# A two-layer hybrid S5 / RetNet / GLA backbone on one core: S5 of the last layer as two streams, a new queue order for the opening, norms rounded straight from PSUM, and SBUF copies in the pack

## The chip, the cores and the metric

One core of a Trainium2 chip runs the whole program in one launch. The metric is device time in microseconds (us). Three runs of the kernel before gave 1385.05, 1386.57 and 1379.94 us, a median of 1385.05 us. The engines are TensorE (PE, matmuls, with PEld as its weight loads), VectorE (DVE), ScalarE (ACT), GpSimd (POOL) and SyncE (SP, which issues most DMAs). Each engine runs its own list of instructions in order, and waits on the others by semaphores.

## The reference, cut to what matters

All numbers are float32. There are 256 context tokens and 256 latent tokens, 1024 channels, two layers:

```python
for l in range(2):
    need_ctx = l < 1                       # the last layer computes no context output
    m_l = split((silu(c) @ w_mod[l] + b_mod[l]), 6);  m_c = split(silu(c_ctx) @ w_mod[l] + b_mod[l], 6)
    p_l = split_in(modulate(rms_norm(x, norm_mix[l]), m_l[0], m_l[1]) @ w_in[l])
    p_c = split_in(modulate(rms_norm(ctx, norm_mix[l]), m_c[0], m_c[1]) @ w_in[l])
    s5_c, s5_l = s5_branch(p_c[0], p_l[0], ...)        # 16 groups of 16 channels, 64 complex states, two directions
    ret_c, ret_l = retnet_branch(p_c[1:5], p_l[1:5], ...)
    gla_c, gla_l = gla_branch(p_c[5:11], p_l[5:11], ...)
    x = x + m_l[2] * (sum_b(sigmoid(p_l[11 + b]) * (y_b @ w_br[b])) @ w_out[l])
    x = x + m_l[5] * swiglu(modulate(rms_norm(x, norm_ffn[l]), m_l[3], m_l[4]), w_ffn_in[l], w_ffn_out[l])
    if need_ctx: ...                                   # the same two steps for ctx
return rms_norm(x, norm_final)
```

Here `modulate(h, shift, scale)` is `h * (1 + scale) + shift`, so no matmul with `w_in[l]` can start before the two rows `m[0]` and `m[1]` are there, which are themselves products with `w_mod[l]`.

## The kernel before, in words

Activations stand transposed in one tile `rb`: 128 channels of a group by tokens, four token tiles of 128 (two of context, two of latent). Every float32 product is made of three matmuls (`mm3`): each operand is split into a high part `hi` (a rounding copy on ACT) and a low part `lo` (a subtraction on DVE), and hi*hi, hi*lo and lo*hi are added up in a PSUM bank `b`. Weights come as 512 KB tiles `raw` by DMA from SP, are split on ACT and DVE into `hi` and `lo`, and go to PE. A line of the profile names the helper that issued an instruction: L243 is `mm_` (matmul), L253 a transpose on PE, L228 `act`, L231 `tt` (two tensors), L234 `stt`, L238 and L240 `ts`, L593 the copy `perm` of the pack, L273 the weight DMA. The pools hand out buffers; a tile framework with priorities decides in which order each engine's instructions stand, so one edit can move others.

The parts that the change touches, in the order of time:

**The opening (0 to 65 us).** `mod_chunk(c)` computes the shift and scale for 256 of the 1024 channels, in four chunks: two DMAs of 1 MB of `w_mod`, 64 matmuls with 32 columns held in PE (`b<-arena,sil`), a copy of the rows on ACT, a transpose, and three small DVE operations. `norm_chunk(c)` transposes those channels of the four normalised token tiles (8 transposes), and multiplies and adds on DVE (four operations of 128x512), rounds on ACT (one copy of 128x1024) and subtracts on DVE (128x1024) to fill `rb`. `pack_mms(c)` then multiplies with one chunk of the weights `w_in` that feed S5's input and the GLA and RetNet q and k: 24 matmuls of 128x512. The three functions are called for c = 0, 1, 2, 3 in turn. Behind the four chunks come `pack_out`, which copies the four banks (ACT) and writes a permuted copy (`perm`, DVE) that goes out by DMA, `load_params2` and `s5_tables`, small parameter work.

**The pack of layer 1 (around 970 us).** `pack_out(lean=True)` does the same for layer 1; `perm` reads the PSUM bank, and the bank comes free when both the ACT copy and `perm` have read it.

**S5 of layer 1 (970 to 1126 us).** Three generators are woven: `weave("rsg")` calls in turn one step of RetNet (`r`), of S5 (`s`) and of GLA (`g`); in between, `tick`-like steps of the merge gates, large matmul groups on 512 columns, fill PE. `s5_core` works in two halves of 8 groups, one after the other in one generator, with four steps each: load, 16 matmuls of 128x64 (X), rotation, scan and unrotation to the states S (DVE, POOL), read-out of 24 matmuls of 32x128 and ACT copies to `yt`. After the weave `s5_out` transposes `yt` and runs GELU and GLU.

**The norm before the FFN of layer 1 (1183 to 1192 us).** `out_tok` gives the residual rows of two latent token tiles; per tile a square and a mean (ACT), a power (POOL), a scaling (DVE, L238), 8 transposes on PE, then `norm_t`: per half of four transposes two ACT and two DVE affine operations of 128x128 into a float32 tile, one ACT rounding copy of 128x512, one DVE subtraction of 128x512. `ffn_in_tok` then multiplies with `w_ffn_in`, `tok_mms` with both token tiles inside the loop over channels.

## Time and profile before

| | |
|---|---|
| median of three runs | 1385.05 us |
| profiled execution, its own time | 1389.15 us |
| its span, first to last instruction | 1387.1 us |
| mean granted TensorE clock | 0.986 of full |
| PE busy | 1332.2 us (96%) |
| DVE busy | 909.6 us (66%) |
| ACT busy | 579.1 us (42%) |
| DMA engines, mean | 184 GB/s |

The profiled execution took 1389.15 us, 2.05 us more than its span and 4.1 us more than the median of the three runs. PE is busy in 96% of the span, so the whole idle time of PE is 54.9 us; the places where PE stands still, and the few where its clock is halved, are what is left besides the matmuls themselves.

### The profile page before, as it was taken

The numbers are of one execution on the slowest core, as the hardware profiler recorded it, in microseconds if no ns is written. First come the engines' busy times: TensorE is split into PE (matmuls) and PEld (weight loads), VectorE is DVE, ScalarE is ACT, GpSimd is POOL, SyncE is SP. The second block draws the span as 40 slices with busy tenths as digits, with TensorE's granted clock in tenths as the row PEclk, the third lists the DMA queues.
The fourth block names the chain that finished last, engine by engine and source line by source line (L and its number), as shares of the span: only waits on it lengthen the run. The fifth ranks groups of instructions, "written<-read, shape, count | busy, mean of one in ns | idle before, by whom it ended". The sixth has DMA issues, their size and how long they took to land.

```text
span 1387.1 us, 20296 instructions
## 1 busy us (share of the span) xinstructions
PE 1332.2 (96%) x7723; PEld 1082.7 (78%) x7723; DVE 909.6 (66%) x1395; ACT 579.1 (42%) x920; POOL 73.7 (5%) x115
## 2 busy tenths in 40 slices
PE   4899999999999999999999999999999989899997
PEld 3788888777767778788777777898987867788886
DVE  4579682849879665535455687764696688655555
ACT  3367352333432233222222345544456544544453
POOL 3310000002000020000000000000000010000000
PEclk9999999999999999999999999999999989999999
DMA  9743455677877565633333787654655646465653
GB/s 308 205 123 106 153 167 165 228 220 236 280 245 216 200 184 170 215 92 106 119 115 116 250 310 245 197 158 122 181 160 189 199 145 213 149 194 187 213 183 106
DMA packets 202584, 255.63 MB, mean 184 GB/s; under 512 B 20704, under 2 KB 153100, under 8 KB 201976
## 3 DMA queue, kind: packets, MB, share of 16 engines
q1 hardware_dynamic: 189032, 228.05, 52.6%
q10 hardware_dynamic: 10240, 20.39, 4.1%
q0 software_dynamic: 3216, 5.91, 1.7%
q8 instruction: 61, 1.00, 0.3%
q14 instruction: 35, 0.29, 0.1%
HBM read 231.00 MB, written 23.30 MB: 183 GB/s over the span
## 4 chain that ended last, share of the span: by engine, by line
PE 81%; DMA 8%; DVE 5%; issue 2%; ACT 2%; SPq 1%; POOL 0%; DVEq 0%; ACTq 0%; POOLq 0%
PE b L243 79%; DMA wm<-in_w_mod_dram 4%; PE b L253 2%; DVE arena L231 1%; DVE zone L234 1%; DVE lo L231 1%; DMA arena<-in_w_mod_dram 1%; DMA raw<-in_w_in_dram 1%; ACT arena L228 1%; DMA arena<-udr 1%; ACT hi L228 1%; DMA arena<-sw 1%; DMA arena<-in_ctx_dram 0%; DMA raw<-in_w_ffn_out_dram 0%; DMA rb<-k 0%
## 5 line engine op out<-in xcount | busy, mean ns | idle before, releaser
L243 PE MATMUL b<-hi,rb 128*128 128x512 f32 (+2 forms) x1752 | 535.5, 383 | 5.5 <-DVE arena L593 3.5
L243 PE MATMUL b<-rb,hi 128*128 128x512 f32 (+1 forms) x1568 | 465.3, 378 | 1.4 <-DVE rb L231 1.4
L231 DVE TENSOR_TENSOR lo<-raw,hi 128x1024 fp32r<-128x1024 f32 (+3 forms) x295 | 333.7, 1136 | 201.4 <-ACT hi L228 198.5
L228 ACT ACTIVATE hi<-raw 128x1024 fp32r<-128x1024 f32 (+3 forms) x295 | 289.7, 989 | 419.4 <-PE b L243 275.0
L243 PEld LDWEIGHTS b<-hi,rb 128*128 128x128 f32 x1752 | 328.1, 189 | 67.4 <-issue 8.1
L243 PE MATMUL b<-lo,rb 128*128 128x512 f32 (+2 forms) x876 | 334.2, 382 | 0.9 <-DVE lo L231 0.9
L243 PEld LDWEIGHTS b<-rb,hi 128*128 128x128 f32 x1568 | 284.5, 189 | 64.5 <-issue 11.9
L243 PE MATMUL b<-rb,lo 128*128 128x512 f32 (+1 forms) x784 | 294.2, 376 | 0.0
L243 PEld LDWEIGHTS b<-lo,rb 128*128 128x128 f32 x876 | 166.2, 190 | 28.3 <-issue 1.6
L243 PEld LDWEIGHTS b<-rb,lo 128*128 128x128 f32 x784 | 147.9, 189 | 28.6 <-issue 3.4
L228 ACT ACTIVATE arena<-b 128x512 f32<-128x512 f32 (+7 forms) x168 | 79.1, 481 | 106.1 <-PE b L243 71.8
L243 PE MATMUL b<-arena 128*128 128x96 f32 (+9 forms) x1056 | 120.7, 289 | 0.8 <-ACT arena L228 0.8
L231 DVE TENSOR_TENSOR arena<-arena 128x512 f32<-128x512 f32 (+5 forms) x164 | 102.0, 640 | 17.2 <-ACT arena L228 14.9
L243 PEld LDWEIGHTS b<-arena 128*128 128x128 f32 (+6 forms) x1056 | 89.9, 160 | 24.3 <-issue 8.3
L234 DVE SCALAR_TENSOR_TENSOR arena<-arena,b 128x512 f32<-128x512 f32 (+1 forms) x124 | 72.3, 587 | 47.4 <-PE b L243 44.3
L234 DVE SCALAR_TENSOR_TENSOR zone<-wm,sil,zone 128x1024 f32<-128x1024 f32 x56 | 71.0, 1280 | 26.1 <-DMA wm<-in_w_mod_dram 26.0
L231 DVE TENSOR_TENSOR zone<-zone 128x512 f32<-128x512 f32 (+3 forms) x117 | 67.9, 604 | 28.5 <-DMA wb<-zone 17.4
L228 ACT ACTIVATE rb<-arena 128x256 fp32r<-128x256 f32 (+3 forms) x101 | 46.4, 476 | 61.5 <-PE b L243 33.6
L231 DVE TENSOR_TENSOR rb<-arena,rb 128x256 fp32r<-128x256 f32 (+2 forms) x106 | 53.7, 521 | 16.9 <-ACT rb L228 16.7
L253 PE MATMUL b<-cst,arena 128*128 128x128 f32 (+2 forms) x254 | 40.0, 284 | 19.4 <-DMA arena<-in_norm_mix_dram 8.9
L253 PEld LDWEIGHTS b<-cst,arena 128*128 128x128 f32 (+2 forms) x254 | 30.9, 146 | 27.3 <-issue 16.1
L228 ACT ACTIVATE arena<-arena 128x512 f32<-128x512 f32 (+3 forms) x62 | 36.7, 599 | 34.9 <-DVE arena L231 27.8
(145 smaller groups left out, 686.5 us busy)
## 6 DMA issues: line engine op xcount, KB each, us to landing
wm<-in_w_mod_dram SPq DMA_DIRECT2D x80, 512.0 KB
raw<-in_w_ffn_out_dram SPq DMA_DIRECT2D x66, 512.0 KB
raw<-in_w_in_dram SPq DMA_DIRECT2D x48, 512.0 KB
raw<-in_w_ffn_in_dram SPq DMA_DIRECT2D x44, 512.0 KB
raw<-in_w_ffn_in_dram SPq DMA_DIRECT2D x88, 256.0 KB
raw<-in_w_in_dram SPq DMA_DIRECT2D x48, 384.0 KB
raw<-in_w_out_dram SPq DMA_DIRECT2D x16, 512.0 KB
arena<-in_w_mod_dram SPq DMA_DIRECT2D x7, 1024.0 KB
```

Source lines behind the costliest of these rows:

```text
L228: self.S.activation(out, in_, f, bias=bias, scale=scale)
L231: self.last = self.V.tensor_tensor(out=out, in0=a, in1=b, op=op).ins
L234: self.last = self.V.scalar_tensor_tensor(out=out, in0=a, scalar=s, in1=b, op0=op0, op1=op1).ins
L243: self.last_mm = self.P.matmul(out, l, r, start=start, stop=stop, **k).ins
L253: self.last_tr = self.P.transpose(out, in_, self.ident[:k, :k]).ins
```

## The change

Five edits, with what the new order shows.

1. Opening. `w_mod` of a chunk comes as four DMAs of 512 KB, by halves of the contraction. `norm_chunk` rounds `rb` on ACT straight from the PSUM bank (`Identity` with scale and shift, four operations of 128x2x128 per chunk), makes the float32 value a second time on DVE (four `tensor_scalar` of 128x2x128) and subtracts in two operations of 128x512. `pack_mms` of a chunk is written behind `norm_chunk` of the next one, and the splitting of a chunk's weights may not stand ahead of the row copy on ACT. `load_params2` must follow the last pack matmul, and `s5_tables` that and the last norm operation on ACT.
2. `norm_t` in the same manner: 16 ACT operations and 16 DVE operations of 128x128 in place of 8, 8 and 4 copies of 128x512.
3. `pack_out` of layer 1: `perm` reads the copy in SBUF that ACT has made, and ACT copies 64x256 of the first bank as well.
4. `s5_core` takes a list of halves; in layer 1 the weave has two S5 streams, `"rstg"`, the second starting three rounds late. Temporaries of the second half lie in another arena.
5. `ffn_in_tok`, first block: per token tile all matmuls with the high part of the activations, then those with the low part.

```diff
@@ mod_chunk
-            self.q["modc"].dma_start(out=ws[m].ap, in_=i["w_mod"][0][:, D * m + 256 * c:D * m + 256 * c + 256].rearrange(
-                "(k p) c -> p k c", p=128))
+        for kh in range(2):
+            for m in (1, 0):
+                self.q["modc"].dma_start(out=ws[m].ap[:, 4 * kh:4 * kh + 4], in_=i["w_mod"][0][
+                    512 * kh:512 * kh + 512, D * m + 256 * c:D * m + 256 * c + 256].rearrange("(k p) c -> p k c", p=128))
...
         self.act(rows.ap, b[:, :128], AF.Copy)
+        self.row_out = self.last_act
@@ norm_chunk
-            self.tt(hv, b.rearrange("p (t k c) -> p t k c", t=2, k=2), bc(self.mod[:, 0, 1]), ALU.mult)
-            self.tt(hv, hv, bc(self.mod[:, 0, 0]), ALU.add)
-        self.act(self.rb[:, 1:5, 0, ks], h32.ap, AF.Copy)
-        self.tt(self.rb[:, 1:5, 1, ks], h32.ap, self.rb[:, 1:5, 0, ks].bitcast(F32), ALU.subtract)
+            for k in range(2):
+                kk = 2 * c + k
+                src = b[:, 256 * k:256 * k + 256].rearrange("p (t c) -> p t c", t=2)
+                self.act(self.rb[:, rows, 0, kk], src, AF.Identity, scale=sc[:, kk, s:s + 1], bias=sh[:, kk, s:s + 1])
+                self.ts(h32.ap[:, :, k], src, sc[:, kk, s:s + 1], sh[:, kk, s:s + 1], ALU.mult, ALU.add)
+            self.tt(self.rb[:, rows, 1, ks], h32.ap, self.rb[:, rows, 0, ks].bitcast(F32), ALU.subtract)
@@ norm_t
-                if k < 2:
-                    self.act(dst, src, AF.Identity, scale=sc[:, kk, s:s + 1], bias=sh[:, kk, s:s + 1])
-                else:
-                    self.ts(dst, src, sc[:, kk, s:s + 1], sh[:, kk, s:s + 1], ALU.mult, ALU.add)
-            self.act(self.rb[:, 1 + t, 0, ks], h32.ap[:, ks], AF.Copy)
+                self.act(self.rb[:, 1 + t, 0, kk], src, AF.Identity, scale=sc[:, kk, s:s + 1], bias=sh[:, kk, s:s + 1])
+                self.ts(h32.ap[:, kk], src, sc[:, kk, s:s + 1], sh[:, kk, s:s + 1], ALU.mult, ALU.add)
@@ pack_out
-            perm(up.ap[:, c0:], banks[x][:, c0:])
+            if lean and x == 0:
+                self.act(o.ap[0:64, 0:256], banks[0][0:64, 0:256], AF.Copy)
+            perm(up.ap[:, c0:], (o.ap if lean else banks[x])[:, c0:])
...
-                perm(up.ap[0:64, 0:256], banks[0][0:64, 0:256])
+                perm(up.ap[0:64, 0:256], o.ap[0:64, 0:256])
@@ s5_core
-    def s5_core(self, l, d, u_dr, t0):
+    def s5_core(self, l, d, u_dr, t0, hfs=(0, 1)):
...
-            rr, ri, t = big.new(8, 64), big.new(8, 64), big.new(8, 64)
+            tmp = self.zone if l and hf else big
+            rr, ri, t = tmp.new(8, 64), tmp.new(8, 64), tmp.new(8, 64)
@@ ffn_in_tok
-                self.tok_mms(banks, ws, (1, 0), range(KD), 0, KD - 1, h)
+                for t in (1, 0):
+                    for k in range(KD):
+                        for x in range(2):
+                            self.mm_(banks[t], h(t, k)[0], ws[k // 2][x][:, k % 2], k == 0 and x == 0, False)
+                    for k in range(KD):
+                        self.mm_(banks[t], h(t, k)[1], ws[k // 2][0][:, k % 2], False, k == KD - 1)
@@ layer
-                    self.pack_mms(banks, self.pack_weights(0, 0, c), c)
+                    with self.tc.issue_after(self.row_out):
+                        ws.append(self.pack_weights(0, 0, c))
+                    if c:
+                        self.pack_mms(banks, ws[c - 1], c - 1)
+                self.pack_mms(banks, ws[3], 3)
...
-        self.weave(("srg", "rsg")[l], g=gla, s=self.s5_core(l, self.s5d[l], u_dr, t0),
-                   r=self.ret(l, rqk, rv, ro, t0))
+        core = lambda *hfs: self.s5_core(l, self.s5d[l], u_dr, t0, hfs)
+        if last:
+            self.weave("rstg", g=gla, s=core(0), t=self.late(3, core(1)), r=ret)
```

ACT in the opening, before: `b_343` and `b_437` are the banks of mod rows of chunks 2 and 3, `hi_501` is the pack weight of chunk 3, `rb` the rounded activations of chunks 2 and 3.

```order
L228 ACTIVATE hi_501<-raw_498 128x16x48
L228 ACTIVATE hi_501<-raw_498 128x16x16
L228 ACTIVATE arena<-b_343 128x128
L228 ACTIVATE hi_639<-raw_636 128x832
L228 ACTIVATE hi_683<-raw_680 128x832
L228 ACTIVATE arena<-b_437 128x128
L228 ACTIVATE rb<-arena 128x4x256 x2
```

ACT in the same place now: the row copies are `arena<-b_331` (chunk 2) and `arena<-b_431` (chunk 3), the pack weight of chunk 3 is again `hi_501`, and `b_478`, `b_488` hold the transposed tokens of chunk 3.

```order
L228 ACTIVATE arena<-b_331 128x128
L228 ACTIVATE hi_401<-raw_398 128x16x48
...
L228 ACTIVATE rb<-b_388,mod 128x2x128
L228 ACTIVATE arena<-b_431 128x128
L228 ACTIVATE hi_501<-raw_498 128x16x48
L228 ACTIVATE hi_501<-raw_498 128x16x16
L228 ACTIVATE hi_663<-raw_660 128x832
L228 ACTIVATE hi_707<-raw_704 128x832
L228 ACTIVATE rb<-b_478,mod 128x2x128
L228 ACTIVATE rb<-b_488,mod 128x2x128
L228 ACTIVATE hi_750<-raw_747 128x832
L228 ACTIVATE rb<-b_478,mod 128x2x128
```

The row copies of chunks 2 and 3 moved ahead of the weight of chunk 3, and one weight of the next product (`hi_750`) stands between the rounding operations of chunk 3.

PE in the opening, before: `b_437` are the mod rows of chunk 3, `b_477` to `b_489` the transposes of chunk 3, `hi_407` the pack weight of chunk 2, `hi_501` that of chunk 3.

```order
L253 MATMUL b_383<-cst,arena 128x128
...
L243 MATMUL b_437<-zone,sil 32x128 x2
L253 MATMUL b_477<-cst,arena 128x128
L253 MATMUL b_482<-cst,zone 128x128 x4
L253 MATMUL b_489<-cst,arena 128x128 x4
L243 MATMUL b_151<-rb,hi_407 128x512
...
L243 MATMUL b_154<-rb,lo_408 128x512
L243 MATMUL b_151<-rb,hi_501 128x512
```

PE in the same place now: `b_431` are the mod rows of chunk 3, `hi_401` is the pack weight of chunk 2, `b_473` to `b_488` the transposes of chunk 3, `hi_501` the pack weight of chunk 3.

```order
L243 MATMUL b_431<-zone,sil 32x128 x2
L243 MATMUL b_151<-rb,hi_401 128x512 x2
L243 MATMUL b_151<-rb,lo_402 128x512
...
L243 MATMUL b_154<-rb,hi_401 128x512 x2
L253 MATMUL b_473<-cst,arena 128x128
L253 MATMUL b_478<-cst,zone 128x128 x4
L253 MATMUL b_488<-cst,arena 128x128 x4
L243 MATMUL b_154<-rb,lo_402 128x512
L243 MATMUL b_154<-rb,hi_401 128x512 x2
L243 MATMUL b_154<-rb,lo_402 128x512
L243 MATMUL b_151<-rb,hi_501 128x512
```

The pack of chunk 2, which stood behind the transposes of chunk 3, now stands ahead of them but for its last four matmuls.

PE at the end of S5 in layer 1, before: `b_8486` and `b_8516` are GLA, `b_8508` and `b_8512` RetNet, `b_9217` a merge gate, `b_8544` the read-out of the second half, `b_8574` the transposes of `yt`.

```order
L243 MATMUL b_8512<-arena 128x128 x2
L243 MATMUL b_9217<-hi_9239,rb 128x512 x2
L243 MATMUL b_9217<-lo_9240,rb 128x512
L243 MATMUL b_9217<-hi_9239,rb 128x512
L243 MATMUL b_8516<-arena 128x96
L243 MATMUL b_8516<-arena 64x96 x4
L243 MATMUL b_8544<-rb,arena 32x128 x4
L243 MATMUL b_8516<-arena 128x96 x2
L243 MATMUL b_8516<-arena 64x96 x4
L243 MATMUL b_8516<-arena 128x96
L243 MATMUL b_8544<-rb,arena 32x128 x20
L253 MATMUL b_8574<-cst,arena 128x64 x4
```

PE in the same place now, from the last gate matmuls: `b_9243` is the merge gate, `b_8490` and `b_8494` the last round of GLA, `b_8512` to `b_8552` RetNet, `b_8570` the read-out of the second half.

```order
L243 MATMUL b_9243<-hi_9265,rb 128x512
L243 MATMUL b_8490<-arena 128x256 x2
L243 MATMUL b_8494<-arena 128x96 x2
L243 MATMUL b_8512<-arena 128x128 x2
L243 MATMUL b_8494<-arena 128x96 x6
L243 MATMUL b_8516<-arena 128x128 x2
...
L243 MATMUL b_8552<-arena 128x128 x2
L243 MATMUL b_8556<-arena 128x96
L243 MATMUL b_8556<-arena 64x96 x4
L243 MATMUL b_8570<-rb,arena 32x128 x4
L243 MATMUL b_8570<-rb,zone 32x128 x4
```

The read-out's place among the GLA matmuls is the same; what moved is the rest: the X matmuls of the second half, which stood about 100 wide gate matmuls behind the read-out of the first half, follow it directly, and the last round of GLA and RetNet has no gate matmuls left in between.

## Rows read from the trace of the kernel before

**Rows 1.** The page: busy us of each engine (share of the span) and instructions.
```profile
PE 1332.2 (96%) x7723; PEld 1082.7 (78%) x7723; DVE 909.6 (66%) x1395; ACT 579.1 (42%) x920; POOL 73.7 (5%) x115
```
**Rows 2.** Waits of PE: waiting line <- awaited: us, times, longest.
```profile
PE b L253 <- ACT arena L228: 4.9, 4, 2.5
PE b L243 <- DVE arena L231: 4.7, 3, 3.0
PE b L253 <- DVE arena L238: 4.2, 2, 2.4
PE b L243 <- DVE zone L234: 2.8, 2, 2.2
```
**Rows 3.** Windows of the opening: us; PE, PEld, DVE, ACT, POOL; PEclk; DMA; GB/s.
```profile
17.70:27.00 9.30, 6.74 (x146) 5.84 (x146) 5.41 (x11) 3.29 (x6) 4.58 (x9) 1.00 1.11 349
27.00:44.90 17.90, 15.41 (x133) 11.62 (x130) 7.40 (x15) 4.03 (x9) 9.60 (x19) 0.99 1.10 337
44.90:51.60 6.70, 6.34 (x81) 4.94 (x81) 5.54 (x12) 2.09 (x4) 2.97 (x6) 0.53 0.72 223
54.90:65.10 10.20, 10.19 (x45) 8.47 (x46) 5.28 (x11) 3.95 (x7) 2.04 (x4) 1.00 0.42 124
```
**Rows 4.** The chain that ended last, opening: start, us, what.
```profile
32.70 10.81 DMA raw<-in_w_in_dram
```
**Rows 5.** Timeline of the opening, ACT: start, us, instruction, idle before.
```profile
43.54 1.15 ACT L228 ACTIVATE hi<-raw 128x768 fp32r<-128x768 f32 x2 [7.21 <-DMA raw<-in_w_in_dram]
44.59 0.26 ACT L228 ACTIVATE arena<-b 128x128 f32<-128x128 f32 x1
```
**Rows 6.** Timeline of the opening, PE.
```profile
44.90 0.48 PE L253 MATMUL b<-cst,arena 128*128 128x128 f32 x1 [2.47 <-ACT arena L228]
54.91 0.50 PE L243 MATMUL b<-rb,hi 128*128 128x512 f32 x1 [1.02 <-DVE rb L231]
```
**Rows 7.** Groups by shape, 900 to 925 us: count, busy us, mean ns.
```profile
L240 DVE TENSOR_SCALAR arena<-b,mod 128x256 f32<-128x256 f32 x8 | 4.0, 540 | 2.2 <-ACT rb L228 2.1
L228 ACT ACTIVATE rb<-b,mod 128x256 fp32r<-128x256 f32 x8 | 4.0, 568 | 6.1 <-PE b L253 4.9 <-DVE arena L240 1.2
L231 DVE TENSOR_TENSOR rb<-arena,rb 128x512 fp32r<-128x512 f32 x4 | 2.7, 684 | 0.0
```
**Rows 8.** Windows across the kernel, columns as in rows 3.
```profile
208.10:277.40 69.30, 69.30 (x503) 52.55 (x501) 36.17 (x68) 20.57 (x32) 1.08 (x2) 1.00 0.62 197
762.90:832.30 69.40, 69.25 (x362) 53.64 (x362) 51.06 (x60) 28.77 (x43) 0.00 (x0) 1.00 0.82 280
```
**Rows 9.** Timeline of the pack of layer 1.
```profile
970.50 0.37 ACT L228 ACTIVATE arena<-b 128x256 f32<-128x256 f32 x1
971.18 0.74 DVE L593 COPY arena<-b 128x256 f32<-128x256 f32 x2
972.06 0.41 PE L243 MATMUL b<-hi,rb 128*128 128x384 f32 x1 [1.70 <-DVE arena L593]
```
**Rows 10.** Timeline of PE at the end of S5.
```profile
1121.86 1.93 PE L243 MATMUL b<-rb,arena 128*32 128x128 f32 x32 [3.00 <-DVE arena L231]
1125.44 1.12 PE L253 MATMUL b<-cst,arena 64*128 64x64 f32 x8 [1.66 <-ACT arena L228]
```
**Rows 11.** The window ahead of it, columns as in rows 3.
```profile
1110.00:1118.80 8.80, 8.80 (x82) 6.52 (x80) 8.16 (x12) 2.21 (x4) 0.00 (x0) 1.00 0.27 67
```
**Rows 12.** Timeline of DVE: one earlier round of GLA's state updates.
```profile
1092.49 1.36 DVE L234 SCALAR_TENSOR_TENSOR arena<-arena,ebl,b 128x96 f32<-128x96 f32 x4
```
**Rows 13.** Timeline of the norm before the FFN of layer 1.
```profile
1188.07 0.56 POOL L491 TENSOR_TENSOR st<-st,mh 128x1 f32<-128x1 f32 x1 [2.47 <-DVE st L240]
1189.12 0.74 DVE L238 TENSOR_SCALAR arena<-arena,st 128x1024 f32<-128x1024 f32 x1
1190.01 1.94 PE L253 MATMUL b<-cst,arena 128*128 128x128 f32 x8 [2.41 <-DVE arena L238]
1191.61 0.78 PE L243 MATMUL b<-hi,rb 128*128 128x512 f32 x1
```

More of the change, by code (lines that the diff above doesn't have):

```diff
@@ L227, in act @@
     def act(self, out, in_, f, scale=1.0, bias=0.0):
-        self.S.activation(out, in_, f, bias=bias, scale=scale)
+        self.last_act = self.S.activation(out, in_, f, bias=bias, scale=scale).ins
     def tt(self, out, a, b, op):
@@ L406, in weave, with late @@
                         del gens[c]
+    @staticmethod
+    def late(n, gen):
+        for _ in range(n):
+            yield
+        yield from gen
     def aside(self, name, gen):
@@ L462, in norm_chunk @@
         ks = slice(2 * c, 2 * c + 2)
-        h32 = self.new(4, 2, 128)
+        sh, sc = self.mod[:, 0, 0], self.mod[:, 0, 1]
         for s in range(2):
             b = self.bank()
-            for t in range(2):
-                for k in range(2):
-                    o = 128 * (2 * t + k)
-                    self.transpose(b[:, o:o + 128], xs[2 * s + t].ap[:, 128 * (2 * c + k):128 * (2 * c + k) + 128])
-            hv = h32.ap[:, 2 * s:2 * s + 2]
-            bc = lambda a: a[:, None, ks, s:s + 1].to_broadcast([128, 2, 2, 128])
-            self.tt(hv, b.rearrange("p (t k c) -> p t k c", t=2, k=2), bc(self.mod[:, 0, 1]), ALU.mult)
-            self.tt(hv, hv, bc(self.mod[:, 0, 0]), ALU.add)
-        self.act(self.rb[:, 1:5, 0, ks], h32.ap, AF.Copy)
-        self.tt(self.rb[:, 1:5, 1, ks], h32.ap, self.rb[:, 1:5, 0, ks].bitcast(F32), ALU.subtract)
-        self.drop(h32)
+            h32 = self.new(2, 2, 128)
+            rows = slice(1 + 2 * s, 3 + 2 * s)
+            for k in range(2):
+                for t in range(2):
+                    o = 128 * (2 * k + t)
+                    self.transpose(b[:, o:o + 128], xs[2 * s + t].ap[:, 128 * (2 * c + k):128 * (2 * c + k) + 128])
+            for k in range(2):
+                kk = 2 * c + k
[3 more added lines that the diff above has]
+            self.tt(self.rb[:, rows, 1, ks], h32.ap, self.rb[:, rows, 0, ks].bitcast(F32), ALU.subtract)
+            self.drop(h32)
+        self.norm_act = self.last_act
     def gate_rows(self, gd):
@@ L1077, in s5_core @@
         nn = 64 - n0
-        u8 = self.new(16, 64)
-        for hf in range(2):
+        for hf in hfs:
+            u8 = self.new(8, 64)
             gs = slice(8 * hf, 8 * hf + 8)
@@ L1128, in s5_core @@
                 self.tt(ri.ap, X[1].ap, b_, ALU.mult)
-                o = self.new(8, 64)
+                o = big.new(8, 64) if x else tmp.new(8, 64)
                 nc.vector.memset(o.ap[0:64, :, 0:1], 0.0)
@@ L1148, in s5_core @@
             self.read_out = self.last_mm
-            if hf == 0:
-                yt = self.yt = self.new(8, 128)
+            if hf == hfs[0] and hfs[0] == 0:
+                self.yt = self.new(8, 128)
+            yt = self.yt
             for gg in range(ng):
@@ L1518, in layer @@
                     self.norm_chunk(c, xs)
-                    self.pack_mms(banks, self.pack_weights(0, 0, c), c)
+                    with self.tc.issue_after(self.row_out):
[3 more added lines that the diff above has]
+                self.pack_mms(banks, ws[3], 3)
                 self.drop(*xs)
+            pe, act = self.last_mm, self.norm_act
             gqk = self.pack_out(0, banks, u_dr)
-            self.load_params2()
+            with self.tc.issue_after(pe):
+                self.load_params2()
         else:
```

17 lines of the change are left out of this document (10 added, 7 removed).

## The prediction, made before the changed kernel ran

> **What bounds the kernel now.** I read the page first, then the waits of PE, then windows and timelines at each long wait. The page says PE is busy 1332.2 us [rows 1], 54.9 us short of the span of 1387.1. No matmul is added or taken away, so the change can only shorten PE's waits, or the stretches in which its clock is halved, or lengthen them. The waits of PE name the places [rows 2]: the row copy on ACT (4.9 us in four waits), the states of S5 (L231, 4.7), the scaled rows of the norm (L238, 4.2), the modulation vectors that DVE adds up (L234, 2.8). The changed lines touch the first three and the pack's copy, not the fourth.
>
> **The opening.** PE runs out of work at 44.90 - 2.47 = 42.43 and waits for the row copy of chunk 2 [rows 6]. That copy takes 0.26 us but stands on ACT behind the splitting of chunk 3's pack weights, which waits 7.21 us for its DMA, until 43.54 [rows 5]; the chain of waits passes through that DMA, landing at 43.51 [rows 4]. [...] The changed order puts the row copy ahead of the splitting and 20 of chunk 2's 24 pack matmuls between the mod rows and the transposes of chunk 3. Step by step: at 42.43 PE has the mod rows of chunk 3 before it; their `w_mod` is issued ahead of the raw tile that landed at 43.51, so I take 43.5 for it. 64 narrow matmuls at full clock take about 1 us, for in the slow stretch of 6.70 us they shared the time with transposes and copies: 44.5. The 20 pack matmuls take 4.5 us: 49.0. The transposes of chunk 3 about 0.8, the four pack matmuls left over 0.9: 50.7, so the transposed tokens are there from about 50.2. Then DVE needs four operations of 0.54 us, one weight subtraction of 128x832 that the new order puts between them, and two subtractions of 128x512 in 0.684 us each [rows 7]; at their rate of 1.3 ns a column the weight takes about 1.0: 2.2 + 1.0 + 1.4 = 4.6, the first subtraction done at 54.1. PE has four matmuls with high parts until 51.6, waits 2.5 us, and needs 20 x 0.2265 = 4.5 more: about 58.7 against 65.0, a gain of 6.3 us. The best that the same work allows, without that wait, is 2.5 us more; but if the mod rows' data came no sooner than before the half-speed stretch ended, two thirds would be gone. I take -6.2 us, between -8.5 and -2. In the new form ACT rounds in four operations of 0.568 us where it had one of 1.06, and they wait for nothing but the transposes, so with one weight between them it finishes at about 53.5; this lies beside DVE's 4.6.
>
> [...]
>
> From 65 to 107 us PE does not wait, so these 6.2 us move the rest of the program forward, unless a later wait was bound by something that does not move. The candidates are the two waits for L234 of 2.8 us in all [rows 2].
>
> **The pack of layer 1.** PE waits 1.70 us until 972.06 for a bank [rows 9]. The bank is free once the second permuted copy, of 64x256, has read it, at 971.18 + 0.74 = 971.92. Now ACT alone frees it: its copy ends at 970.87, the added one of 64x256 follows directly, ending at about 971.2. Gain 0.7 us, between 0 and 1.1. What is late next is that ACT copy; the permuted copies come later, but only the transfer of u waits for them.
>
> **S5 of layer 1.** PE waits 3.00 us before the read-out of the second half, for the states that DVE makes, and 1.66 us behind it for the ACT copies of `yt` [rows 10]. DVE is full in the stretch ahead, 8.16 of 8.80 us [rows 11], against 66% over the span [rows 1]. With the second stream entering three rounds late, X of the second half comes right behind the first read-out, about 100 wide matmuls (23 us) ahead of the second, and the states' operations move into time in which DVE had room. The 3.00 us go. What is late next: GLA's last round, which has no gate matmuls left to hide behind. Between two of its products DVE does six state updates of 1.36 / 4 = 0.34 us [rows 12], a small copy and one operation of 128x512 (0.68, as in [rows 7]), by estimate 3.0 us, where PE has about ten matmuls or 2.3 us; then a weight subtraction of 128x1024 and four small predicated copies, again some 3 us by estimate, beside about 2.5 us of PE. I put 0.7 and 0.6 us of new waits there. The 1.66 us for `yt` stay. So -1.7 us, between -5 (the 3.00, and the half-speed stretch behind it too) and +1.5 (GLA's chain, now delayed by the states' operations ahead of it, waits longer than 3.00).
>
> **The norm and the FFN's start.** The second tile's power ends at 1188.63, but its scaling begins only at 1189.12, because DVE does affine operations of the first tile; the transposes start at 1190.01 and the FFN at 1191.61 [rows 13]. In the new order both scalings stand ahead of the affine operations, and the FFN of one tile needs only its high part, made by ACT from PSUM. The first tile gets ready later, since more matmuls of the second tile stand ahead of it on PE; the second 0.5 to 1 us sooner; the first FFN matmul one rounding operation after its transposes instead of affine, copy and subtraction. I take -1.5 us, between -3.5 and +1. The 16 operations of 128x128 on ACT replace 8 and 4 copies, about equal in time.
>
> **The sum.** -6.2 - 0.7 - 1.7 - 1.5 = -10.1 us. `load_params2` and `s5_tables` cost nothing in it: the work on DVE stood behind the last pack matmul before, too, and the waits of their small DMAs lie on POOL. The reordered queues of layer 0 get no value and +-3 us. Against the profiled execution's 1389.15 this makes 1379. The median of the runs before was 1385.05, 4.1 us lower; the time to compare is thus 1385.05 - 10.1 = 1375 us.
>
> **Rivals.** First, the opening's gain is given back. For it: the waits for L234 hang on DMAs of `w_mod` that are issued when buffers come free, and 2.8 us were waited there [rows 2]. Against it: those buffers are freed by DVE behind PE's own work, which moves too. If it loses two thirds, -6.2 becomes -2 and the sum is -5.9: 1379 us.
>
> Second, S5 and the norm only change what they wait for: DVE does as much as before, and the 4.7 and 4.2 us of [rows 2] stay under other names. Against it: DVE's room ahead of the read-out. The sum is then -6.9: 1378 us. Both together come to -2.7: 1382 us, no change.
>
> Third, slower: the halved `w_mod` transfers starve the opening. From 17.70 to 44.90 the DMA engines moved 9.30 us x 349 + 17.90 us x 337 GB/s, 9.3 MB, at full share [rows 3]. Should smaller pieces bring only the 197 GB/s of a stretch fed by 512 KB tiles [rows 8], the same bytes take 47 us instead of 27.2, 20 us more; less 10.1 that is +10: 1395 us. It decides below 9.3 MB / (27.2 + 10.1 us) = 249 GB/s. Against it: that stretch used only 0.62 of the engines' time, and another with 512 KB tiles reached 280 GB/s at 0.82, 341 per full share [rows 8], where the opening had 306 to 314 [rows 3].
>
> [...]
>
> Last, the restrained order itself may fail to do what it says: if another weight split still stands ahead of chunk 3's row copy, only the smaller terms are left, -3.9: 1381 us. The new order on ACT speaks against it.
>
> **How the numbers follow.** My forecast gets 0.60, the first rival 0.10, the second 0.12, both together with the failing order 0.12, the third 0.06. A measurement of this kernel can tell about 0.5%, 7 us, from no change. Around the forecast the bounds of the terms add up to -21 at best and +3 at worst, but they seldom fall together: its own range is 1367 to 1381. To hold 8 in 10 over all cases I take 1366 to 1385. Faster by over 7 us (below 1378) gets most of the forecast and half of the first two rivals, 0.68; within 0.5% the rest of these, 0.25; slower 0.07.
>
> **What would show it right or wrong.** Right: no wait of PE for the row copy near 42 us, the last pack matmul of the opening at about 59 us and not 65, the 3.00 us wait before the read-out gone, less than 1 us at the pack, the first FFN matmul 1 to 2 us sooner behind the output projection, and the same distance between 107 and 960 us. Wrong: PE waiting for `w_mod` transfers beyond 45 us, a half-speed stretch in GLA's last round, or longer waits for L234 near 400 and 515 us.

## The result, and the profile after

The kernel got slower: 1405.6 us median (1402.18 to 1408.44) against 1386.2 for the kernel before beside it, ratio 1.0141, 95% interval 1.011 to 1.0172. The profiled execution took 1402.8 us, 13.65 more than that of before. The forecast was 1375 us, in a range of 1366 to 1385. Here and below, ratios leave out the executions that lie over 1.5% above the fastest of their kernel.

Busy time and instructions of each engine, from the page of the changed kernel:

```profile
PE 1345.3 (96%) x7723; PEld 1091.7 (78%) x7723; DVE 912.8 (65%) x1407; ACT 586.4 (42%) x940; POOL 74.8 (5%) x115
```

Beside [rows 1] this is the main reading: PE has the same 7723 matmuls and 13.1 us more busy time, while its idle time (span 1400.6 less 1345.3) is 55.3 us, against 54.9 before. So on balance the loss is not in waits but in matmuls at half clock, that is at 0.5 of full, the lower of the two levels (1 and 0.5) that the records of the granted clock show in both traces. They show it for some 39 us of the span before, and 61 after. Two stretches make the difference: 1004.8 to 1018.4, new, and 1117.4 to 1141.3, where before it was 1119.6 to 1129.9.

Following the same matmul through both traces gives the account by place. The changed kernel is 2.75 us ahead at 77 us; even (+0.1) at 461; 3.0 ahead again at 972, after two short waits near 843 that are gone; even at 992; 9.6 behind at 1012, 12.4 at 1064, 12.0 at 1126, 11.8 at 1183, 13.55 from 1235 to the end.

Two cautions on accounts by place. The medians are 19.4 us apart, the two profiled executions only 13.65; the traces do not show where the rest lies. And executions differ though their lists do not. In the runs below, eleven kernels have PE's list of before to 240 us and beyond; at 100 us all eleven stand 1.1 to 2.0 us ahead of the profiled execution of before. Six of them have it to 930 us, and at 900 these stand 0.3 to 7.8 us ahead. So places are best compared over short stretches, and a lead of 1 or 2 us at one place shows little.

**Opening.** PE of the changed kernel around the last pack chunk (start, duration, engine, line, operation, tiles, count, idle time before and its releaser); it answers to [rows 6]:

```profile
51.33 1.10 PE L243 MATMUL b<-rb,hi 128*128 128x512 f32 x4
55.84 0.78 PE L243 MATMUL b<-rb,hi 128*128 128x512 f32 x1 [3.41 <-DVE rb L231]
56.41 0.63 PE L243 MATMUL b<-rb,lo 128*128 128x512 f32 x1
```

and DVE there:

```profile
52.65 1.03 DVE L231 TENSOR_TENSOR lo<-raw,hi 128x832 fp32r<-128x832 f32 x1 [0.89 <-ACT hi L228]
53.59 0.99 DVE L240 TENSOR_SCALAR arena<-b,mod 128x256 f32<-128x256 f32 x2
54.50 1.28 DVE L231 TENSOR_TENSOR rb<-arena,rb 128x512 fp32r<-128x512 f32 x2
```

The row copy no longer holds PE at 42 us. But the wait of 3.41 us lasts until both subtractions are done, and the matmuls behind it run at half clock to 59.3: 0.63 us for one, where at full clock one takes 0.40. The last pack matmul ends at about 62.1, against 65.0 before. In the eleven other executions of the opening of before it ends between 63.0 and 63.9, so 0.9 to 1.8 us are the gain beside those.

**Behind layer 0's gates.** Waits of the changed kernel between 385 and 420 us (engine, line, what ended the waits: us in total, times, longest):

```profile
DVE zone L234 <- DMA wm<-in_w_mod_dram: 9.0, 6, 4.2
PE b L243 <- DVE rb L231: 4.6, 1, 4.6
```

PE waits 4.6 us for DVE to make `rb`, and DVE's sums wait before that for tiles of `w_mod`, 9.0 us in six waits. In [rows 2] these sums cost PE 2.8 us. The clock falls within this wait and is at half from 407.5 to 414.3. By 461 nothing is left of the opening's gain.

**1000 to 1020 us.** Windows of both kernels; columns are the window, its length, then busy us (instructions) of PE, PEld, DVE, ACT and POOL, the granted clock, DMA share, GB/s. Before:

```profile
1000.00:1010.00 10.00, 9.22 (x64) 8.58 (x63) 6.64 (x14) 5.35 (x9) 0.00 (x0) 1.00 0.86 245
1010.00:1020.00 10.00, 10.00 (x66) 8.49 (x65) 9.54 (x18) 6.61 (x10) 0.00 (x0) 1.00 0.52 160
```

After:

```profile
1000.00:1010.00 10.00, 5.94 (x30) 5.56 (x29) 5.59 (x13) 3.01 (x5) 0.00 (x0) 0.74 1.01 243
1010.00:1020.00 10.00, 10.00 (x41) 9.10 (x41) 6.33 (x13) 7.89 (x12) 0.00 (x0) 0.58 0.43 151
```

30 matmuls in place of 64, with the DMA engines full; then 41 in place of 66 in the same busy time, at a clock of 0.58. What stands in the way, of the changed kernel on SP, ACT, DVE and PE:

```profile
990.76 5.91 SPq L1106 DMA_DIRECT2D arena<-k  x5
999.38 0.39 SPq L273 DMA_DIRECT2D raw<-in_w_in_dram  x1
...
996.44 0.85 ACT L228 ACTIVATE hi<-raw 128x768 fp32r<-128x768 f32 x1 [5.41 <-DMA raw<-in_w_in_dram]
1003.49 0.84 ACT L228 ACTIVATE hi<-raw 128x768 fp32r<-128x768 f32 x1 [6.20 <-DMA raw<-in_w_in_dram]
...
1004.36 0.96 DVE L231 TENSOR_TENSOR lo<-raw,hi 128x768 fp32r<-128x768 f32 x1 [5.16 <-ACT hi L228]
1005.71 0.42 DVE L231 TENSOR_TENSOR arena<-b,arena 128x256 f32<-128x256 f32 x1
...
1006.17 7.09 PE L243 MATMUL b<-arena,zone 128*128 128x64 f32 x32 [4.06 <-DVE arena L231]
```

S5's loads (`k`, `rot`, `wc`, `wb`) and the tiles of `w_in` share SP's queue. A tile comes late, its rounding waits on ACT, its subtraction on DVE, and behind that stands RetNet's rotation (1005.71), which reads the bank that S5's X matmuls are to write. PE waits 4.06 us, the clock falls in that wait (1004.8), and the X block then takes 7.09 us at half clock; before it took 3.77 with no wait:

```profile
1001.37 3.77 PE L243 MATMUL b<-arena,zone 128*128 128x64 f32 x32
```

**S5's end** (answers to [rows 10]):

```profile
1115.46 14.52 PE L243 MATMUL b<-arena 48*128 48x256 f32 x70 [2.34 <-DVE arena L234]
...
1137.49 1.11 PE L253 MATMUL b<-cst,arena 64*128 64x64 f32 x8 [1.63 <-ACT arena L228]
```

The 3.00 us for S5's states are gone, as foreseen. In their place stand 2.34 us in front of the last RetNet and GLA products, 70 narrow matmuls with no gate matmul between them, at half clock from 1117.4 on.

**The norm** (answers to [rows 13]): one wait in place of two. The first line is before's first wait, which [rows 13] does not have, the others are the changed kernel's.

```profile
1186.54 1.06 PE L253 MATMUL b<-cst,arena 128*128 128x128 f32 x8 [1.79 <-DVE arena L238]
...
1200.65 2.79 PE L253 MATMUL b<-cst,arena 128*128 128x128 f32 x12 [4.13 <-DVE st L240]
1203.09 0.78 PE L243 MATMUL b<-hi,rb 128*128 128x512 f32 x1
```

PE stands still for 4.13 us, 1.79 + 2.41 = 4.20 before. Half clock lasts 6.8 us in both.

### The profile page after: what moved, and what is told of

Its sections match the earlier page's. It is cut to its first block, busy times and chain, and to the rows that moved or that the text cites. A ratio compares the mean times of both kernels' runs of the same rounds, so it can differ in the third digit from the quotient of the medians.

```text
span 1400.6 us, 20309 instructions
## 1 busy us (share of the span) xinstructions
PE 1345.3 (96%) x7723; PEld 1091.7 (78%) x7723; DVE 912.8 (65%) x1407; ACT 586.4 (42%) x940; POOL 74.8 (5%) x115
## 4 chain that ended last, share of the span: by engine, by line
PE 78%; DMA 8%; DVE 6%; issue 4%; ACT 2%; SPq 0%; POOL 0%; DVEq 0%; ACTq 0%; POOLq 0%
PE b L243 76%; DMA wm<-in_w_mod_dram 3%; PE b L253 2%; DVE zone L234 2%; DMA arena<-in_w_mod_dram 1%; DVE lo L231 1%; DMA raw<-in_w_in_dram 1%; DVE arena L231 1%; ACT arena L228 1%; DMA arena<-rot 1%; ACT hi L228 1%; DMA arena<-in_x_dram 1%; DVE zone L231 1%; DMA raw<-in_w_br_s_dram 0%; DVE arena L709 0%
## 5 line engine op out<-in xcount | busy, mean ns | idle before, releaser
L228 ACT ACTIVATE hi<-raw 128x1024 fp32r<-128x1024 f32 (+3 forms) x295 | 289.5, 988 | 405.3 <-PE b L243 298.5
L231 DVE TENSOR_TENSOR lo<-raw,hi 128x1024 fp32r<-128x1024 f32 (+3 forms) x295 | 334.2, 1138 | 186.2 <-ACT hi L228 182.9
L243 PE MATMUL b<-arena 128*128 128x96 f32 (+8 forms) x1064 | 128.4, 299 | 3.2 <-DVE arena L234 2.3
L228 ACT ACTIVATE arena<-b 128x256 f32<-128x256 f32 (+7 forms) x170 | 79.4, 480 | 111.3 <-PE b L243 84.5
L243 PEld LDWEIGHTS b<-arena 128*128 128x128 f32 (+5 forms) x1064 | 97.0, 168 | 28.0 <-issue 12.0
L231 DVE TENSOR_TENSOR arena<-arena 128x512 f32<-128x512 f32 (+4 forms) x162 | 102.0, 645 | 10.5 <-ACT arena L228 8.1
L234 DVE SCALAR_TENSOR_TENSOR arena<-arena,b 128x512 f32<-128x512 f32 (+1 forms) x124 | 72.5, 588 | 51.1 <-PE b L243 49.5
L234 DVE SCALAR_TENSOR_TENSOR zone<-wm,sil,zone 128x1024 f32<-128x1024 f32 x56 | 70.9, 1281 | 31.4 <-DMA wm<-in_w_mod_dram 30.6
L231 DVE TENSOR_TENSOR zone<-zone 128x512 f32<-128x512 f32 (+4 forms) x122 | 70.7, 605 | 27.5 <-DMA wb<-zone 18.2
L231 DVE TENSOR_TENSOR rb<-arena,rb 128x256 fp32r<-128x256 f32 (+1 forms) x110 | 54.2, 505 | 14.5 <-ACT rb L228 14.2
L228 ACT ACTIVATE rb<-arena 128x256 fp32r<-128x256 f32 (+3 forms) x93 | 39.8, 443 | 52.3 <-PE b L243 40.6
L253 PEld LDWEIGHTS b<-cst,arena 128*128 128x128 f32 (+2 forms) x254 | 31.5, 147 | 24.3 <-issue 14.4
L228 ACT ACTIVATE arena<-arena 128x512 f32<-128x512 f32 (+3 forms) x62 | 37.0, 601 | 29.8 <-DVE arena L231 20.1
```

The costliest lines, as they stand in the source:

```text
L228: self.last_act = self.S.activation(out, in_, f, bias=bias, scale=scale).ins
L231: self.last = self.V.tensor_tensor(out=out, in0=a, in1=b, op=op).ins
L234: self.last = self.V.scalar_tensor_tensor(out=out, in0=a, scalar=s, in1=b, op0=op0, op1=op1).ins
L243: self.last_mm = self.P.matmul(out, l, r, start=start, stop=stop, **k).ins
L253: self.last_tr = self.P.transpose(out, in_, self.ident[:k, :k]).ins
```

## Experiments

Ratios are to the kernel before on the same chip. Edits are numbered as in the section on the change.

**Undoing or isolating one edit.**

Without edit 3:

```diff
-            perm(up.ap[:, c0:], (o.ap if lean else banks[x])[:, c0:])
+            perm(up.ap[:, c0:], banks[x][:, c0:])
```

> The changed kernel without its pack edit (perm reads PSUM again, no added ACT copy), all else kept. Theory A: the pack edit moved RetNet's second rotation on DVE behind two more weight subtractions, so that S5's first X matmuls waited 4.1 us for a bank and PE's clock fell; then the stretch from 985 to 1020 us loses some 12.6 us less, X starts without a wait, and the time is 1386 to 1394 us, within 0.5% of before. Theory B: the two S5 streams did it, their loads standing ahead of a weight on SP; then the wait and the half-speed stretch stay and the time stays at 1400 to 1406.

1407.1 us, 1.0159 (1.0129 to 1.019): not cured. PE still waited 4.3 us, from 1004.1, now for ACT (L228), with half clock 1006.6 to 1013.4 and 1112.4 to 1139.7. Theory A, that edit 3's order on DVE is the only cause, falls.

Edit 3 alone (the same diff, reversed, on the kernel before):

> The kernel before with the pack edit alone. Theory A: 9 to 13 us slower than before, with the wait of about 4 us ahead of S5's X matmuls and a half-speed stretch behind it; PE's 1.70 us wait at the pack itself gone. Theory B: 0.7 us faster, no wait at X.

1399.4 us, 1.0095 (1.006 to 1.013): 2.8 us of waits between 1002 and 1007, half clock 1007.3 to 1024.4, and 11 us lost there. A few copies in the pack, forecast at -0.7 us, do that.

Edit 4 alone (`s5_core` in two streams, `"rstg"`):

> The kernel before with the two S5 streams alone. Theory A: the 3.0 us wait for the states goes, but the last round of GLA and RetNet, now without wide matmuls, runs at half clock for some 24 us where it was 10; net 1 to 4 us slower, X unhindered at 1000 us. Theory B: 10 us slower, with the wait at X. The prediction's own figure was 1.7 us faster.

1400.5 us, 1.0103 (1.0062 to 1.0144). The same place again, by another route:

```profile
1009.05 1.22 PE L243 MATMUL b<-arena 48*128 48x128 f32 x4 [4.02 <-ACT arena L228]
```

Edits 3 and 4 alone cost 13 and 14 us. They do not add up: each loses its time at the same place, and beside the others edit 3 adds nothing that can be told, as the run without it shows.

Edit 1 alone (`w_mod` in halves, the norm rounded from PSUM, the new order):

> The kernel before with the opening alone (pieces of w_mod, rounding from PSUM, pack matmuls a chunk later). From the changed kernel's trace: the last pack matmul at 62.1 and not 65.0 us, and of these 2.9 us nothing left at 470 us because the queues of layer 0 stand otherwise. Expected 0 to 3 us faster at 850 us and at the end. If the loss behind 110 us comes from the other edits instead, 3 us faster at 470 already.

1395.3 us, 1.0069 (1.0038 to 1.01). 1.7 us ahead at 80 us (no more than the other executions of before's opening), 2.0 behind at 480: PE waits 4.7 us for `rb` (L231) at 406, and half clock lasts 6.8 us there against 3.4. Its trace is 3.6 us behind at the end, so most of the 0.69%, 9.6 us, is not placed.

**Is it the loads, the clock, or the order?** All of PE's, DVE's and ACT's instructions stay in the changed kernel's order, but S5's loads that are needed 100 us later leave SP's queue:

```diff
-            self.q["s5"].dma_start(out=wc.ap, in_=d["wc"][:, :, gs])
...
+            mark = self.G.tensor_copy(self.mh[0:1, 8:9], X[1].ap[0:1, 0, 0:1]).ins
+            with self.tc.issue_after(mark):
+                self.q["misc"].dma_start(out=wc.ap, in_=d["wc"][:, :, gs])
```

> The changed kernel, with S5's layer-1 loads of wc and k (2 x 1 MB and 16 x 64 KB) issued from POOL after the 16 X matmuls of their half, in place of from SP ahead of them; the lists of PE, DVE and ACT are the same row for row. Theory L (the burst of S5 loads on SP's queue delays the w_in tile between them; ACT and DVE stand behind that tile, PE behind DVE): the 4.1 us wait of PE at 1001.8 shrinks below 1 us, the half-clock stretch 1004.8 to 1018.4 goes, time 8 to 11 us below the changed kernel, about 1.006 of before. Theory R (the row order alone sets the loss; the tile is late because its buffer comes free late): the wait stays at 3 us or more, the half clock too, time within 2 us of the changed kernel, 1.014 of before.

1394.7 us, 1.0072 (1.0047 to 1.0098): the ratio is 0.7% lower, 9.6 us, as Theory L said. The lists of PE, DVE and ACT are the changed kernel's row for row, so its order is not what made this part of the loss; between 990 and 1030 us of it, 9.9 us come back. The loads were both delayed and given to POOL's queue; which of the two did it was not separated. PE at the X block, and S5's end:

```profile
1007.42 3.73 PE L243 MATMUL b<-arena,zone 128*128 128x64 f32 x32
...
1109.30 9.38 PE L243 MATMUL b<-arena 48*128 48x256 f32 x70 [0.63 <-DVE arena L234]
```

No wait, and 3.73 us for X in place of 7.09. ACT still waits for such tiles, but less:

```profile
ACT hi L228 <- DMA raw<-in_w_in_dram: 6.7, 2, 5.2
```

in two waits, for 14.4 us in four. The narrow block gained too, 9.38 us for 14.52, with its wait shrunk to 0.63. What is left of the loss, 1.0072, is the size of edit 1's, 1.0069.

Ten useless wide matmuls in the wait at 1113:

```diff
+                    if left == 3:
+                        for z in range(10):
+                            self.mm_(banks[0], self.zr, w[0][:, z % 2], False, False)
```

> The changed kernel with ten more 128x512 matmuls, whose stationary operand is zero, standing exactly in PE's wait of 2.34 us at 1113 (row order before it unchanged); they add work and nothing to the result. Clock theory (PE's waiting among narrow matmuls is what brings the half clock): the wait at 1113 is filled, the 70 narrow matmuls behind it take about 8 us in place of 14.5, the half-clock stretch 1117 to 1141 shrinks to 10 us or less, time 6 to 9 us below the changed kernel. Rival (the narrow form itself brings it): the clock falls some us later all the same, gain 0 to 3 us, or a loss of up to 2.3 us, what ten wide matmuls take.

1403.0 us, 1.0101 (1.0058 to 1.0144).

```profile
1118.73 2.43 PE L244 MATMUL b<-hi,zr 128*128 128x512 f32 x10
1121.09 9.03 PE L244 MATMUL b<-arena 48*128 48x256 f32 x70
```

The block is 5.5 us shorter for work that does nothing, and half clock begins only at its end, 1130.1. The block did what the clock theory said; that half clock came all the same behind it, until 1143.8, is what the rival said. Of 5.5 us gained over the block 4.3 are left at 1178. On the whole the ratio is 0.4% lower, which the two intervals do not part from nothing; 6 to 9 us were expected.

The order alone, on the kernel before:

```diff
-        self.weave(("srg", "rsg")[l], ...
+        self.weave(("srg", "rgs")[l], ...
```

> The kernel before, with one thing changed: in layer 1 the rounds of the weave call RetNet, GLA, S5 in place of RetNet, S5, GLA. No work is added, removed or loaded otherwise. Theory R (the order before is one that happens to stand well; any other costs, as waits of 2 to 4 us among narrow matmuls bring half clock): 4 to 14 us slower, with a new half-clock stretch of over 7 us between 1000 and 1145. Rival (the loss belongs to the S5 streams and the pack copies themselves): within 4 us of before.

1396.9 us, 1.0068 (1.0039 to 1.0098), within Theory R's range. The profiled execution took 1409.9 us, 13 us above the median, so it shows where this order can lose, and not how much a usual execution loses there. New half clock stands from 1014.5 to 1031.6, and at S5's read-out:

```profile
1136.71 0.65 PE L243 MATMUL b<-rb,arena 128*32 128x128 f32 x8 [6.14 <-DVE arena L231]
1141.99 1.93 PE L243 MATMUL b<-rb,arena 128*32 128x128 f32 x32 [4.62 <-DVE arena L231]
```

S5's states are waited for twice in this execution, 10.8 us in place of 3.00. Two letters changed places, no work was added or removed, and it cost half of what the change cost.

Edits 2 and 5 alone:

> The kernel before with edits 2 and 5 alone (norm_t rounded from PSUM, first FFN block by high and low parts). The prediction's term: -1.5 us (-3.5 to +1). What the changed kernel's trace shows (one wait of 4.1 us of PE in front of the FFN for two of 2.4 and 1.0, with 12 transposes at half clock): +1 to +3 us, all of it between 1183 and 1235.

1386.6 us, 0.9998 (0.9976 to 1.0021): no change that can be told. The -1.5 us forecast and the +1.8 seen between 1183 and 1235 in the changed kernel both lie in the interval.

**Cures.** The kernel before, its two waits at S5's end filled (12 and 5 zero matmuls):

> The kernel before with 17 matmuls of 128x512 whose stationary operand is zero: 12 where PE waits 3.00 us ahead of S5's read-out (1118.9 to 1121.9) and 5 where it waits 1.66 us ahead of the transposes of yt (1125.4); nothing else moves on PE up to there, the result is the same. Clock theory: at 0.23 us each they fit the waits, the half-clock stretch 1119.6 to 1129.9 shrinks to under 4 us or goes, read-out, transposes and the wide matmuls behind run at full clock: 2 to 4 us faster, 0.997 to 0.9985 of before. Rival (the half clock there has another reason): the stretch stays, and they cost 0 to 2 us.

1387.3 us, 1.0018 (0.9997 to 1.0039): near the rival's number, but not by its mechanism.

```profile
1115.13 3.01 PE L244 MATMUL b<-rb,zr 128*128 128x512 f32 x12
...
1131.33 2.04 PE L244 MATMUL b<-arena 128*128 128x256 f32 x4 [3.91 <-issue]
...
1126.51 1.22 DVE L232 TENSOR_TENSOR lo<-raw,hi 128x1024 fp32r<-128x1024 f32 x1
1128.55 1.23 DVE L232 TENSOR_TENSOR lo<-raw,hi 128x1024 fp32r<-128x1024 f32 x1 [0.15 <-ACT hi L229]
1129.93 0.96 DVE L232 TENSOR_TENSOR arena<-arena,hn 128x768 f32<-128x768 f32 x1 [0.16 <-POOL hn L893]
1130.81 0.75 DVE L235 SCALAR_TENSOR_TENSOR arena<-arena 128x256 f32<-128x256 f32 x2
```

The half clock of 1119.6 to 1129.9 is gone; two of 3.4 us each stand in its place, 1110.3 to 1113.7 and 1130.8 to 1134.2. But then PE stands 3.91 us before the GLU's product (`128x256 x4`). The view names nothing that it waits for; by DVE's rows it is the last step of GELU (1130.81). In front of that step now stand two subtractions of weights and an operation of GLA (0.96), which came behind it before: the added matmuls moved DVE's order as well. So what the clock alone is worth here stays open.

Late loads, no edit 1, zero matmuls 3 and 5:

> The changed kernel without the opening's edits, with S5's wc and k loads of layer 1 behind the X matmuls (as in the run of the late loads), and with zero matmuls in the waits at S5's end (3 ahead of the last RetNet scores, 5 ahead of the transposes of yt). If the three causes add up (loads on SP's queue 10 us, narrow tail at half clock 4 to 5, opening's later loss 3.6), it comes out within 2 us of before, 1 to 2 us below it at best. If the row order alone is what costs: 5 us or more above before, with new waits between 1000 and 1045.

1393.6 us, 1.0039 (1.0012 to 1.0067), 5.4 us: outside the first account's 2 us, and in the second's range, but without its new waits: PE has none between 996 and 1046. Three were too few, a wait of 1.34 stayed, and the five ran at half clock, 2.50 us in a wait of 1.63.

The same without zeros:

> The changed kernel without the opening's edits, S5's wc and k loads of layer 1 behind the X matmuls, no zero matmuls; lists of PE, DVE and ACT as in the changed kernel without the opening. Account: of the changed kernel's 1.014, the loads' 10 us and the opening's 3.6 us are gone, left are S5's narrow end at half clock (about 14 us of it against 10 before: 2 us) and the norm's 0: 1.000 to 1.003 of before, no PE wait over 1 us between 1000 and 1030. Rival (pack copies and streams cost by themselves, whatever the loads do): 1.005 or more.

1389.1 us, 1.0015 (0.9985 to 1.0045): the account holds, no PE wait between 996 and 1030. With the early loads and edit 1 both gone, what is left of the 1.41% cannot be told from nothing; edits 2 to 5 are all in. S5's end is now at half clock from 1103.7 to 1131.0.

With nine zeros in the one wait ahead of the block:

> The kernel of the late loads without the opening's edits, with nine zero matmuls of 128x512 in the wait of 1.89 us ahead of the last RetNet scores (1100.4 to 1102.3), where the first zeros worked, and none elsewhere. In the run without them the 70 narrow matmuls behind that wait took 14.94 us and the clock was at half from 1103.7 to 1131.0. Clock account: 9 to 10 us for the 70, the stretch shorter by 8 us or more, 3 to 5 us less on the whole: 0.998 to 0.999 of before. Rival (what the clock gives back returns as a wait for GELU, as in the kernel before with zeros): the 70 at full clock, but the total within 1.5 us of the run without, 1.000 to 1.003.

1390.0 us, 1.0026 (0.9998 to 1.0053).

```profile
1102.03 2.38 PE L244 MATMUL b<-arena 48*128 48x256 f32 x12
1105.04 11.19 PE L244 MATMUL b<-arena 128*128 128x96 f32 x58 [0.62 <-DVE arena L235]
```

The wait was filled and the clock fell nevertheless, at 1105.9, after 0.62 us without work inside the block. The total lies in the rival's range, but not by its mechanism, so neither account holds: filling the wait ahead is not enough to keep the clock through this block.

Edit 4 alone with late loads:

> The kernel before with edit 4 alone (two S5 streams) and the wc and k loads of layer 1 behind the X matmuls. Edit 4 alone was 1.010 of before, with a PE wait of 4.0 us at 1005 behind a w_in tile that landed 9.5 us after ACT was free for it. Account: that wait falls below 1 us, half clock 1007.9 to 1025 goes, 8 to 11 us less: 1.001 to 1.004. Rival (the late tile has nothing to do with these loads): the wait stays above 3 us, 1.008 or more.

1392.0 us, 1.0061 (1.0031 to 1.0091), above the 1.001 to 1.004 expected. The wait of 4.0 us at 1005 and the half clock behind it are gone, worth 9.6 us between 980 and 1060 against the run of edit 4 alone; but S5's end keeps 27.3 us at half clock:

```profile
1105.21 15.46 PE L243 MATMUL b<-arena 48*128 48x256 f32 x70 [2.66 <-DVE arena L234]
```

The opening, with the low parts last in chunk 3:

```diff
-                self.pack_mms(banks, ws[3], 3)
+                self.pack_mms_lo_last(banks, ws[3], 3)
```

> The kernel before with edit 1 alone, and in chunk 3 of the opening's pack the 8 matmuls with the low parts of the activations after the 16 with the high parts. If PE's wait of 3.4 us at 55.8 is for the second of the two subtractions, it falls to 1.5 us or less and the last pack matmul ends near 60 in place of 62.1 us; if the rounding itself is late, it stays. On the whole time: the run of edit 1 alone was 1.007 of before; if what the opening gains is given back at 406 us, where PE waits 4.7 us for rb behind w_mod's sums on DVE, this one is at 1.004 to 1.009 as well; if not, 1.5 to 2 us below that run.

1394.8 us, 1.0064 (1.0043 to 1.0085).

```profile
53.34 0.50 PE L243 MATMUL b<-rb,hi 128*128 128x512 f32 x1 [0.29 <-ACT rb L228]
...
55.60 2.12 PE L243 MATMUL b<-rb,hi 128*128 128x512 f32 x8
```

The last pack matmul ends at 57.7, and PE is 7.2 us ahead of before at 106: more than was forecast, and 5.2 to 6.2 ahead of the other executions of that opening. At 480 it is 3.8 behind. DVE there:

```profile
414.32 1.28 DVE L234 SCALAR_TENSOR_TENSOR zone<-wm,sil,zone 128x1024 f32<-128x1024 f32 x1 [4.30 <-DMA wm<-in_w_mod_dram]
415.52 0.69 DVE L231 TENSOR_TENSOR rb<-arena,rb 128x512 fp32r<-128x512 f32 x1
```

The sum over `w_mod` waits 4.30 us for its tile, `rb` stands behind it, and PE waits 3.8 us.

Late loads on the kernel before, alone and with edits 2 and 5:

> The kernel before with S5's wc and k loads of layer 1 moved to POOL behind the X matmuls, as in the run of the late loads; lists of PE, DVE and ACT as before up to one swap at S5's read-out. In before ACT waits 5.0 and 3.7 us for w_in tiles between 996 and 1005, but PE only 0.8. Theory L: those ACT waits shrink by half or more, PE gains its 0.8 us at most: -1 to 0 us. Theory R: no change, within 1 us. Slower by over 2 us would say that the loads now come too late for S5's read-out.

> The kernel before with the wc and k loads of layer 1 behind the X matmuls, and edits 2 and 5 (norm rounded from PSUM, first FFN block by high and low parts), the version that the runs point to. The two alone were 0.998 and 1.000: 0.996 to 1.000 of before, 0 to 5 us faster. Above 1.002 would say that they hinder one another.

1383.0 us, 0.9979 (0.9956 to 1.0002), and 1382.3 us, 0.9978 (0.9953 to 1.0003): neither can be told from no change. The runs point to this last one; it beats the changed kernel by over 1.5%, and is 0.2% below the kernel before, within that interval.

## Why the prediction was wrong, point by point

**The opening, -6.2: mechanism right, two sizes off, and it didn't last.** The row copy, the order and the last chunk came as worked out. The 0.2265 us of a pack matmul is that of [rows 3], 10.19 us for 45. No run shows the 1 us for the 64 matmuls of the mod rows: at a granted clock of 1.00 they took 1.96 us in the kernel before (at 25.11), and 32 of them 1.08 in the changed kernel (at 32.09). Failed: "the first subtraction done at 54.1 ... waits 2.5 us". The first matmul with a low part reads all four token tiles and needs both subtractions, done at 55.8, so PE went on 1.7 us later than worked out; and the matmuls behind ran at half clock to 59.3, another 1.7 us, which had no price. 2.75 us were left. The run with the low parts last undid just that, and the gain came to 7.2. Third, the starting point was one execution: the 6.70 us at a clock of 0.53 [rows 3] that the forecast set out from (half clock from 44.4 to 51.2) were missing in nine of the eleven other executions of that opening and 3.4 us long in two. Beside those 0.9 to 1.8 us of the 2.75 are left.

**"These 6.2 us move the rest of the program forward": failed.** The first rival, given 0.10, came true in full: of three openings (1.7, 2.75 and 7.2 us ahead) nothing was left at 480. Its place was at the sums of `w_mod`, which wait for their DMAs (L234), as the rival said; PE itself waited not for the sums but for `rb` (L231), whose subtractions stand behind them on DVE. Against it I had put that their buffers "are freed by DVE behind PE's own work, which moves too"; the sums' waits for DMA, up to 4.30 us, show that the transfers did not move as much. How much each wait and each slow stretch between 106 and 480 took was not separated.

**The pack, -0.7: right and worth nothing.** The 1.70 us of [rows 9] are gone; but 2.9 us of lead are lost between 972 and 992, among them 1.21 us of a new wait ahead of four transposes at 986.7.

**S5, -1.7: the step that failed most.** The 3.00 us went and the 1.63 us stayed, as foreseen. The waits of "0.7 and 0.6 us" in GLA's last round became one of 2.34. The half-speed stretch there, which I had named only as a sign of error, had no price: 14.52 us against 9.03 at full clock for the same 70 matmuls, 5.5 us. The larger loss, 9.7 us between 992 and 1012 and 2.8 more by 1064, lay where I had not looked: at the start of the weave. There the sum had nothing; the run of the late loads puts the price of S5's early loads at 9.6 us. I read what DVE computes ahead of S5's read-out, but not what SP loads, nor what stands behind a weight's rounding on ACT and DVE when its tile is late. The rows were there: before, too, ACT waited 5.0 and 3.7 us for such tiles, until 1001 and 1005, with the DMA engines at 0.86, and PE lost only 0.78:

```profile
1000.92 0.84 ACT L228 ACTIVATE hi<-raw 128x768 fp32r<-128x768 f32 x1 [5.00 <-DMA raw<-in_w_in_dram]
1005.44 0.84 ACT L228 ACTIVATE hi<-raw 128x768 fp32r<-128x768 f32 x1 [3.67 <-DMA raw<-in_w_in_dram]
...
1008.50 0.71 PE L243 MATMUL b<-arena 48*128 48x128 f32 x4 [0.78 <-ACT arena L228]
```

**The reordered queues, "no value and +-3 us": failed.** This range was set for layer 0 alone; layer 1's order got none at all. The swap of two letters in the weave cost 9 us, as much as the whole gain forecast. One other order was tried, so whether before's is a lucky one stays open; edit 3, which only moves copies, cost 13 us alone.

**The norm, -1.5: nothing that can be told.** The first FFN matmul came 6.57 us behind the last of the output projection (1196.52 to 1203.09), 6.86 before: 0.3 us sooner, where 1 to 2 were forecast. One wait of 4.13 us replaced 1.79 and 2.41: a weight's subtraction on DVE (1.22 us, as before) and now the residual operations of both tiles stood in front of the first tile's scaling. On ACT the 16 operations of 128x128 took 6.4 us, the 8 of them and the 4 copies of 128x512 before 5.6.

**The third rival, halved `w_mod`: did not happen.** PE's waits for `w_mod` up to 24 us fell from 6.2 to 3.8 us, and from 24 to 44 us the DMA engines moved 340 GB/s in both kernels. So this trace shows no loss by the halves, and the first 32 matmuls of chunk 0 started at 14.5 us, on the first half, where all 64 had waited until 17.7.

**What stays open.** What sets the moment at which the clock falls in the narrow block at S5's end. It fell in all nine kernels that have the block: 0.1 to 1.9 us after the block's start in the five with 1.89 to 2.68 us of waiting ahead (14.52 to 16.12 us for the 70 matmuls); 7.6 and 8.4 us after it with 1.34 and 0.63 us of waiting ahead, and 9.0 us, at its end, where zero matmuls filled the wait in the changed kernel. But with the nine zeros, and no wait ahead, it fell after 3.9 us. So a wait ahead goes with an early fall, and the block without one does not keep the clock either. Also open is where most of edit 1's 0.69% is lost.

## What to carry to other kernels

Before moving work in a kernel that is 96% busy, list for each engine what stands behind a weight that may come late, and what else is on its DMA queue at that time: loads needed 100 us later should not stand in front of it (9.6 us here, by the run that both delayed them and changed their queue). Price half clock for narrow matmuls behind a wait, not the wait alone (here 5.5 us on 70 of them, behind a wait of 2.34). Take the starting point from more than one execution. And test a reordering that changes nothing else: its cost is the bar that any edit of the order has to clear.
